# The first stage of a decoder block: eight token blocks side by side in place of five, with the modulation summed on VectorE

## The chip, the cores and the metric

The kernel runs on one core of a Trainium2 chip. A core has TensorE (PE, matrix products into PSUM), VectorE (DVE), ScalarE (ACT), GpSimd (POOL) and SyncE (SP), which here issues the DMAs. The metric is the device time of one execution in microseconds (us). Beside the runs that give the median, one execution was profiled; its trace gives all rows shown here.

## The reference

One decoder block for 1024 tokens with 1024 features, all in float32. This is the part that matters here:

```python
cond = silu(c)
sh_a, sc_a, gt_a, sh_m, sc_m, gt_m = split(cond @ w_ada + b_ada, 6)
h = rms_norm(x, g_attn_pre) * (1 + sc_a) + sh_a
proj = h @ w_in        # 1024 x 2304: q, k, v of two attention mixers
# rotary, sliding-window attention, dilated attention, out projection, gate, residual, then an MLP
```

`cond` is one vector of 1024 numbers, so `cond @ w_ada` for the shift and the scale of the first half of the block is a sum over 1024 rows of 2 x 1024 weights (8 MB). Shift and scale are wanted with the feature index on the partitions, since h is used transposed.

## The kernel before, in words

**Layout.** The tokens are cut into eight blocks (tb) of 128, the features into eight chunks (k) of 128, the columns of `w_in` into six units (u) of 384. Products keep float32 accuracy by a split: each operand is a high part (fp32r) and a low part (the rest), and three products are added: hi·hi, hi·lo (`proj_mm`, `part` 0, L771 and L772) and lo·hi (`part` 1, L774). A block of a unit is thus 24 products of 384 columns into one bank of PSUM. The split of h is `hw`, that of the weights `w_hl`.

**The first stage.** Each block of x is loaded (L449), its sum of squares taken on ScalarE (L553), the root by a pow on GpSimd (L412), x scaled (L558), transposed by eight TensorE products (L568), and copied to `xnT` (L573), features on partitions. `mod_chunk(k)` gets shift and scale of one chunk: the rows of `w_ada` lie eight to a partition, and the eight slices, each times its number of `cond`, are added over j and then over the partitions. For chunk 0 TensorE does all eight slices, for the others two (table `ADA_PE`, narrow products of one column, L615); VectorE adds the other six (`acc_a`, 128x256, L626 and L628), and two narrow products with ones add over the partitions (`pm`, L635). Then `g_a` and `s_a` (L640, L641), the modulation on ScalarE (L645), its high part on ScalarE (L651) and its low part on GpSimd (L654), for the first five blocks (`FIRST`) at once, 128x640. The weights of unit 0 are split on ScalarE (L473) and GpSimd (L478). The last three blocks go another way: their x is loaded when the last condition tiles have been issued, and modulation is done on the transposes (L583).

**Unit 0.** `first_unit` runs chunk by chunk over five blocks in five banks of PSUM, so that a chunk can be used as soon as it is modulated. Blocks 5 to 7 of unit 0 and the other units go block by block (`proj_tile`). Behind each block `evac` empties its bank: v to `v_hl` (L684, L689), rotary (L700 to L704), the split q and k (`sp`, `sk`, L716 and L717), transposed back by products with an identity.

**Behind it.** Attention of the heads already projected is woven into units 1 to 5; then come the out projection (461 to 565 us) and an MLP with seven products of half-size matrices (565 to 1186 us).

**The order.** All instructions come out of a list planner (`Sched`) that runs before the launch: steps with an estimated duration, dependencies, and rings of slots (`Res`) that they take and give. For each engine it picks the step that can start first, so a step's place on its engine follows from these estimates; on TensorE `prefer` ranks the streams. On the chip each engine runs its list in that order.

Of the kernel before, what the change touches and what calls it, by code (L numbers as in the profile page):

```python
# [19 lines left out]
P = 128  # L20
# [114 lines left out]
class Sched:  # L135


    def __init__(self):
        self.clk = dict(PE=0.0, ACT=0.0, DVE=0.0, POOL=0.0, SP=0.0)
        self.queue = {e: [] for e in ("ACT", "DVE", "POOL", "SP")}  # L140
        self.pe = {}
        self.launch = []
        self.seq = 0
        self.dma = 0.0

# [84 lines left out]
    def run(self, prefer):  # L230
        while True:
# [29 lines left out]
            if e == "PE":  # L261
                self.pe[name].pop(0)
# [41 lines left out]
def hybrid_block(ctx: ExitStack, tc: tile.TileContext, x, positions, w_ada, b_ada, g_attn_post, w_in, w_out,  # L304
# [110 lines left out]
    FIRST = 5  # L415
# [4 lines left out]
    xnT = p0.tile([P, KC, FIRST * P], F32, name="xnT")  # L420
    r_wa, r_xs, r_acc = Res(4), Res(2), Res(3)
# [6 lines left out]
    e_c = load(lambda: nc.sync.dma_start(head[:], consts[:, 0:HEAD]), 106496, prio=pri())  # L428
    wa_t, wa_e, sent = {}, {}, {}

    def load_ada(k):
        def emit():
            wa_t[k] = p0.tile([P, KC, 2, P], F32, name="wa", tag="wa", bufs=4)
            for i in range(2):
                nc.sync.dma_start(wa_t[k][:, :, i], ada_view[:, :, i * D + k * P:i * D + (k + 1) * P])

        def issued():
            sent[k].t = 0.0
        sent[k] = Ev()
        wa_e[k] = load(emit, 1048576, takes=[(r_wa, 1)], prio=pri(), after=issued)  # L440
# [3 lines left out]
    def load_x(tb, deps=()):  # L444
        r = r_stg if tb % 2 == 0 else r_xs

        def emit():
            x_t[tb] = stage("x_sb") if tb % 2 == 0 else p0.tile([P, D], F32, name="x_sb", tag="x_sb", bufs=2)
            nc.sync.dma_start(x_t[tb][:], x[tb * P:(tb + 1) * P])  # L449
        x_e[tb] = load(emit, 524288, deps, takes=[(r, 1)], prio=pri())  # L450
# [3 lines left out]
    def load_w(u, k, prio=None, deps=()):  # L454
# [13 lines left out]
        w_rawe[u, k] = load(emit, 196608, deps, takes=[(r_wst, 1)], prio=pri() if prio is None else prio)  # L468

    def split_w(u, k):  # L470
# [10 lines left out]
        if u == 0:  # L481
            w_e[u, k] = op("POOL", t_ptt(UW), lo(G), [e], gives=[(r_wst, 1)], prio=3)
# [3 lines left out]
    for tb in range(2):  # L486
        load_x(tb)
    e_posi = load(lambda: nc.sync.dma_start(posi[:], positions), 4096, prio=pri())
    load_ada(0)
    for tb in range(2, FIRST):  # L490
        load_x(tb)
    load_w(0, 0)
    for k in range(1, KC):
        load_ada(k)
        load_w(0, k)
    for tb in range(FIRST, TB):
        load_x(tb, [sent[KC - 2 if tb == FIRST else KC - 1]])

    e_init = op("DVE", 0.3, lambda: (V.memset(ones[:], 1.0), V.memset(nhalf[:], -0.5)), prio=0)
# [33 lines left out]
    def f_ang():  # L533
        V.tensor_scalar(ang[:], ang[:], 3.1415925, -3.1415925, ALU.min, ALU.max)
        V.tensor_scalar(kq[:], ang[:], -1.0, None, ALU.mult)
        V.tensor_tensor(kq[:], kq[:], ang[:], ALU.max)
        V.tensor_scalar(kq[:], kq[:], -1.0, float(np.pi / 2), ALU.mult, ALU.add)
    e = op("DVE", 0.8, f_ang, [e], prio=8)

    def f_sin():  # L540
# [3 lines left out]
    e = op("ACT", 3.0, f_sin, [e], prio=8)  # L544
    e_rope = op("DVE", 0.15, lambda: V.tensor_scalar(sinw[:, :, 0], sinw[:, :, 1], -1.0, None, ALU.mult), [e],
                prio=8)

    e_xn = []

    def x_block(tb):  # L550
# [8 lines left out]
        box, eh, d_all, evs_ = {}, [], [], []  # L559

        def hv():
            return x_t[tb][:].rearrange("p (k t) -> p k t", k=KC)
        r_x_ = r_stg if tb % 2 == 0 else r_xs
        for g in range(2):
# [4 lines left out]
            d = pe_op("xt", 0.7, tr, [e], takes=[(r_t, 1)], gives=[(r_x_, 1)] if g and tb < FIRST else [])  # L569
            d_all.append(d)  # L570
            if tb < FIRST:
                def ev(fn, g=g):
                    return lambda: fn(xnT[:, 4 * g:4 * g + 4, tb * P:(tb + 1) * P], box[g][:])  # L573
                e_xn.append(op("ACT", t_ps(512), ev(A.copy), [d], gives=[(r_t, 1)], prio=2))
            else:
                def ev(eng, g=g):
                    def f():
                        for k in range(4 * g, 4 * g + 4):
                            if eng is A:
                                A.activation(hv()[:, k], box[g][:, k - 4 * g], AF.Identity,  # L580
                                             bias=s_a[:, k:k + 1], scale=g_a[:, k:k + 1])
                            else:
                                V.tensor_scalar(hv()[:, k], box[g][:, k - 4 * g], g_a[:, k:k + 1],  # L583
                                                s_a[:, k:k + 1], ALU.mult, ALU.add)
                    return f
                evs_.append((d, ev))
        for d, ev in evs_:

            eh.append(op(("ACT", "DVE"), (1.4, 1.3), (ev(A), ev(V)), d_all + [e_gs[k] for k in range(KC)],
                         gives=[(r_t, 1)], prio=1))  # L590
        if tb >= FIRST:
            def hi(fn):
# [1357 lines left out]
```

## Time and profile before

| | |
|---|---|
| median of 3 runs | 1200.22 us (1197.69 to 1201.38) |
| profiled execution | 1197.14 us, span of the trace 1195.4 us |
| TensorE busy in the span | 96% |
| first product of block 5 of unit 0 | 77.18 us |
| first product of unit 2 | 174.97 us |

In the rows, L771 is line 771 of the kernel before; the fields are engine, operation, output<-inputs, shape. PE is TensorE's products, PEld its weight loads, which overlap. Rows of a timeline begin with the start in us and the busy time. Groups end with their count, the busy time and the mean of one in ns, then the idle time ahead of them with what ended it. A product's busy time spans its pipeline; the distance from start to start is its price in a row of products.

### The profile page before, as it was taken

The page shows a single profiled execution, that of the slowest core. Times are in us where ns is not written, and L with a number is a line of the kernel's source. Part 1 is how long each engine was busy: PE and PEld are TensorE (multiplying, and loading weights), DVE is VectorE, ACT ScalarE, POOL GpSimd, SP SyncE. Part 2 cuts the span into 40 slices and gives each one's busy share as a digit, 9 for nine tenths or more (in the row PEclk, how much of TensorE's full clock was granted, in tenths as well). Part 3 has the DMA queues.
Part 4 walks back from the last instruction along what each step waited for, and adds up shares of the span by engine and source line. Part 5 has one row for each costly group of instructions (what it writes and reads, how often), then busy time and mean ns, then how long its engine had stood idle before and what let it go on. Part 6 is the DMA issues. An engine that isn't in the chain of part 4 may idle for free.

```text
span 1195.4 us, 17424 instructions
## 1 busy us (share of the span) xinstructions
PE 1143.5 (96%) x6064; PEld 998.0 (83%) x6064; DVE 881.3 (74%) x1794; ACT 666.6 (56%) x1411; POOL 264.6 (22%) x325
## 2 busy tenths in 40 slices
PE   7879999999998998999899999999999999999996
PEld 6869999989998896888688888888888888888885
DVE  4977667666789897667888955479763797646998
ACT  6457666556666787667657533473325643246542
POOL 6534655465655333111100000000000000000002
PEclk9889999999999999999999999999999999999999
DMA  9621333213231422555296126952268511586103
GB/s 290 189 60 60 89 98 97 77 52 102 76 87 54 125 53 77 179 201 204 113 381 246 36 73 238 340 168 62 81 218 284 191 36 53 179 287 220 36 19 141
DMA packets 104423, 166.53 MB, mean 139 GB/s; under 512 B 11152, under 2 KB 56336, under 8 KB 104336
## 3 DMA queue, kind: packets, MB, share of 16 engines
q1 hardware_dynamic: 104336, 165.42, 41.8%
q8 instruction: 48, 0.79, 0.3%
q14 instruction: 39, 0.32, 0.1%
HBM read 137.08 MB, written 28.31 MB: 138 GB/s over the span
## 4 chain that ended last, share of the span: by engine, by line
PE 76%; DVE 13%; issue 4%; ACT 3%; POOL 3%; DMA 1%; SPq 0%; DVEq 0%; POOLq 0%; ACTq 0%
PE mlp_ps L1773 16%; PE mlp_ps L1774 16%; PE mlp_ps L1772 16%; PE pj L771 4%; PE pj L774 3%; PE pj L772 3%; PE s_ps L997 3%; PE o_ps L1131 1%; PE pt_ps L1100 1%; DVE acc_a L628 1%; PE y_ps L1348 1%; PE y_ps L1350 1%; PE pm L615 1%; PE y_ps L1349 1%; PE pt_ps L1103 1%
## 5 line engine op out<-in xcount | busy, mean ns | idle before, releaser
L1772 PE MATMUL mlp_ps<-hw 128*128 128x512 f32 x896 | 350.4, 391 | 0.4 <-ACT hw L1534 0.4
L1773 PE MATMUL mlp_ps<-hw 128*128 128x512 f32 x896 | 349.2, 390 | 1.1 <-DVE hw L1540 1.1
L1774 PE MATMUL mlp_ps<-hw 128*128 128x512 f32 x896 | 349.1, 390 | 0.0
L1773 PEld LDWEIGHTS mlp_ps<-hw 128*128 128x128 f32 x896 | 168.6, 188 | 36.9 <-DVE hw L1540 1.4
L1772 PEld LDWEIGHTS mlp_ps<-hw 128*128 128x128 f32 x896 | 168.6, 188 | 36.1 <-ACT hw L1534 0.8
L1774 PEld LDWEIGHTS mlp_ps<-hw 128*128 128x128 f32 x896 | 168.5, 188 | 35.1
L1543 DVE TENSOR_TENSOR hw<-w,hw 128x1024 fp32r<-128x1024 f32 x96 | 114.6, 1219 | 93.5 <-ACT hw L1536 93.3
L1536 ACT CAST hw<-w 128x1024 fp32r<-128x1024 f32 x96 | 97.4, 1046 | 129.9 <-PE mlp_ps L1774 93.2
L1872 POOL TENSOR_TENSOR st<-st,nhalf 128x1 f32<-128x1 f32 x8 | 7.8, 978 | 602.8 <-DVE st L1870 602.8
L771 PE MATMUL pj<-w_hl,hw 128*128 128x384 f32 x344 | 128.2, 373 | 10.0 <-DVE sk L717 10.0
L774 PE MATMUL pj<-w_hl,hw 128*128 128x384 f32 x344 | 117.4, 341 | 0.0
L772 PE MATMUL pj<-w_hl,hw 128*128 128x384 f32 x344 | 117.1, 341 | 0.0
L1536 ACT CAST hw<-u 128x1024 fp32r<-128x1024 f32 x48 | 48.6, 1051 | 64.6 <-PE mlp_ps L1774 64.6
L1118 DVE TENSOR_TENSOR ph<-pt_ps,ph 128x512 fp32r<-128x512 f32 (+1 forms) x110 | 68.8, 643 | 18.5 <-ACT ph L1114 17.6
L771 PEld LDWEIGHTS pj<-w_hl,hw 128*128 128x128 f32 x344 | 65.8, 191 | 11.8 <-issue 8.7
L1543 DVE TENSOR_TENSOR hw<-u,hw 128x1024 fp32r<-128x1024 f32 x48 | 57.0, 1217 | 18.2 <-ACT hw L1536 18.2
L1114 ACT CAST ph<-pt_ps 128x512 fp32r<-128x512 f32 (+1 forms) x110 | 59.2, 560 | 13.8 <-PE pt_ps L1103 9.8
L772 PEld LDWEIGHTS pj<-w_hl,hw 128*128 128x128 f32 x344 | 66.2, 192 | 0.8 <-issue 0.2
L774 PEld LDWEIGHTS pj<-w_hl,hw 128*128 128x128 f32 x344 | 65.7, 191 | 0.0
L1027 POOL TENSOR_SCALAR p_sb<-p_sb,den 128x128 f32<-128x128 f32 (+3 forms) x64 | 50.1, 786 | 70.2 <-DVE den L1025 46.8
L1830 DVE TENSOR_TENSOR yacc<-yacc,mlp_ps 128x512 f32<-128x512 f32 x96 | 62.1, 680 | 3.3 <-PE mlp_ps L1774 3.3
L1022 ACT ACTIVATE p_sb<-p_sb,mn 128x128 f32<-128x128 f32 (+3 forms) x64 | 49.9, 780 | 20.4 <-DVE mn L1015 16.6
(209 smaller groups left out, 2202.6 us busy)
## 6 DMA issues: line engine op xcount, KB each, us to landing
hw<-s_dram SPq DMA_DIRECT2D x84, 512.0 KB, 4.5
wa_st<-in_w_ada SPq DMA_DIRECT2D x32, 512.0 KB, 4.0
w<-in_w_up SPq DMA_DIRECT2D x32, 512.0 KB, 5.4
w<-in_w_down SPq DMA_DIRECT2D x32, 512.0 KB, 8.0
s_dram<-hw SPq DMA_DIRECT2D x28, 512.0 KB, 4.3
x_sb<-in_x SPq DMA_DIRECT2D x16, 512.0 KB, 6.2
wa<-in_w_ada SPq DMA_DIRECT2D x16, 512.0 KB, 7.0
w_st<-in_w_in SPq DMA_DIRECT2D x32, 192.0 KB, 4.7
```

The lines of the kernel that those rows point to most:

```text
L771: T.matmul(ps, hw[:, tb, 0, t], w[:, 0], start=(k == 0), stop=False)
L772: T.matmul(ps, hw[:, tb, 0, t], w[:, 1], start=False, stop=False)
L774: T.matmul(ps, hw[:, tb, 1, t], w[:, 0], start=False, stop=(k == KC - 1))
L1027: lambda b=b, qi=qi: G.tensor_scalar(rec.p[qi], rec.p[qi], b["den"][:], 1.0, ALU.mult, ALU.mult), [e], prio=1))
L1114: A.copy(b["ph"][:, 0, :w], b["pt"][:, :w])
L1118: V.tensor_tensor(b["ph"][:, 1, :w], b["pt"][:, :w], b["ph"][:, 0, :w].bitcast(F32), ALU.subtract)
L1536: A.copy(out[j][0], flat(src[j]))
L1543: V.tensor_tensor(out[j][1], flat(src[j]), out[j][0].bitcast(F32), ALU.subtract)
L1772: T.matmul(ps[m][:], sh, mh, start=starts and k == 0, stop=False, **kw)
L1773: T.matmul(ps[m][:], sh, ml_, start=False, stop=False, **kw)
L1774: T.matmul(ps[m][:], sl, mh, start=False, stop=k == 3, **kw)
L1830: e = op("DVE", t_dv(512), lambda: V.tensor_tensor(y(), y(), ps[m][:], ALU.add), [e, ml.e_y[tb, n]], gives=gives, prio=1)
```

## The change

Only the first stage and unit 0 are written anew.

- `FIRST` is 8: all eight blocks of x are loaded early, turned to `xnT`, and accumulate unit 0 side by side in all eight banks of PSUM. The list `order0` sets the order of the loads, and `in_turn` issues each behind the one before.
- The modulation goes by four groups of two chunks. A group has four tiles of 0.5 MB, two j and 2 x 256 columns each; every third of the tiles and x blocks uses the staging ring, the others a ring of six.
- The sums over j are on VectorE alone, 128x512 (L611, L613 of the changed kernel), eight instructions for a group; four narrow products add over partitions (L621). `ADA_PE` and its products are gone.
- ScalarE writes the high part straight from the modulation (L649); VectorE does the modulation again in full (L647) and subtracts (L652). The first group is done in two halves of four blocks, the others over all eight, 128x1024.
- The weights of unit 0 are split on VectorE in place of GpSimd. GpSimd keeps the steps of the rotary angle, the pow, and six low parts of unit 1's weights. The rest of the angle follows behind the x blocks.
- `filler` puts products of 128x512 ones into TensorE's list where the planner sees it idle, until block 4 (`FILL`), whose bank they write, begins; its first product starts the sum anew.
- Unit 0 runs over seven blocks for chunks 0 to 5 (`AHEAD` is 6), then block 7 for these, then each block's chunks 6 and 7. The weights of unit 1 are loaded as soon as the first stage's loads are out.

```diff
-    FIRST = 5
+    FIRST = 8
+    AHEAD = 6
+    order0 = [("x", 0), ("x", 1)] + [(0, j) for j in range(4)] + [("x", t) for t in range(2, 4)] + [("w", 0), ("w", 1)] + [("x", t) for t in range(4, TB)] + [a for g in range(1, 4) for a in [(g, j) for j in range(4)] + [("w", 2 * g), ("w", 2 * g + 1)]]
...
         if u == 0:
-            w_e[u, k] = op("POOL", t_ptt(UW), lo(G), [e], gives=[(r_wst, 1)], prio=3)
+            w_e[u, k] = op("DVE", t_dv(UW), lo(V), [e], gives=[(r_wst, 1)], prio=3)
...
+    def mod_group(g):
+        b = {}
+        e = e_cond
+        c = slice(2 * g, 2 * g + 2)
+        for j in range(4):
             def f(j=j):
...
+                for n in range(2):
+                    w, cj = wa_t[g, j][:, 512 * n:512 * n + 512], cond[:, 2 * j + n:2 * j + n + 1]
+                    if j == n == 0:
+                        b["acc"] = p0.tile([P, 512], F32, name="acc_a", tag="acc_a", bufs=2)
+                        V.tensor_scalar(b["acc"][:], w, cj, None, ALU.mult)
+                    else:
+                        V.scalar_tensor_tensor(b["acc"][:], w, cj, b["acc"][:], ALU.mult, ALU.add)
...
+        for half in ((0, 1) if g == 0 else (None,)):
+            for k in range(2 * g, 2 * g + 2):
+                mod_chunk(k, eg, half)
+        for k in range(2 * g, 2 * g + 2):
+            split_w(0, k)
...
+        eh = op("ACT", t_sb(n) + 2 * AP_COST, lambda: A.activation(hh, h, AF.Identity, bias=s_a[:, k:k + 1],
+                                                                  scale=g_a[:, k:k + 1]), deps, prio=0)
+        e = op(("DVE", "ACT"), (t_d2(n) + 2 * AP_DV, t_sb(n) + 2 * AP_COST), (full(V), full(A)), [eh], prio=0)
+        e = op("DVE", t_dv(n), lambda: V.tensor_tensor(hw[:, t0:t1, 1, ks], h, hh.bitcast(F32), ALU.subtract), [e],
+               prio=0)
...
-    acc_at = [(pj, "pj", r_pj)] * 2 + [(po, "o", r_o)] + [(psp, "s", r_s)] * 2
+    acc_at = [(pj, "pj", r_pj)] * 2 + [(po, "o", r_o)] + [(psp, "s", r_s)] * 2 + [(pt, "t", r_t)] * 2 + [(px, "x", r_x)]
...
+    def filler(start, o):
+        if fill.open or e_init.t is None:
+            return
+        idle = start - max(sc.clk["PE"], e_init.t + 0.2)
+        n = int(max(0.75 * idle, 0.5 * min(o.dur, 2.0)) / 0.22)
+        for _ in range(n):
+            T.matmul(accs[FILL][:], ones_r[:, :P], ones_r[:], start=True, stop=True)
+        sc.clk["PE"] += max(0.0, 0.22 * n - max(0.0, idle))
...
     def first_unit():
+        order = [(k, part, tb) for x in (0, 1) for k in range(2) for part in range(2)
+                 for tb in (range(4) if x == 0 else range(4, 7))]
+        order += [(k, part, tb) for k in range(2, AHEAD) for part in range(2) for tb in range(7)]
+        order += [(k, part, 7) for k in range(AHEAD) for part in range(2)]
+        order += [(k, part, tb) for tb in (7, 0, 1, 2, 3, 4, 5, 6) for k in range(AHEAD, KC) for part in range(2)]
```

The order of VectorE's instructions in the sums, before, about two chunks (`acc_a` the sums, `pm` the totals, `bb` the bias):

```order
L626 TENSOR_SCALAR acc_a<-wa,cond 128x256
L640 TENSOR_SCALAR g_a<-pm,bb,head 128x1
L641 TENSOR_SCALAR s_a<-pm,bb 128x1
L628 SCALAR_TENSOR_TENSOR acc_a<-wa,cond,acc_a 128x256 x3
L620 TENSOR_TENSOR bb<-bb,pm 128x2
L628 SCALAR_TENSOR_TENSOR acc_a<-wa,cond,acc_a 128x256 x2
```

And VectorE at the end of the changed first stage, from the middle of the last group's sums (`w_hl` the weight splits, `xnT` the modulation, `hw` the low parts, chunk 4's first):

```order
L613 SCALAR_TENSOR_TENSOR acc_a<-wa,cond,acc_a 128x512 x2
L509 TENSOR_TENSOR w_hl<-w_st,w_hl 128x384
L647 TENSOR_SCALAR xnT<-xnT,g_a,s_a 128x1024
L613 SCALAR_TENSOR_TENSOR acc_a<-wa,cond,acc_a 128x512 x2
L652 TENSOR_TENSOR hw<-xnT,hw 128x8x128 x2
L627 TENSOR_TENSOR g_a<-pm,bb 128x2
L628 TENSOR_TENSOR g_a<-g_a,head 128x2
L629 TENSOR_TENSOR s_a<-pm,bb 128x2
L509 TENSOR_TENSOR w_hl<-w_st,w_hl 128x384 x2
...
L647 TENSOR_SCALAR xnT<-xnT,g_a,s_a 128x1024 x2
L652 TENSOR_TENSOR hw<-xnT,hw 128x8x128 x2
```

The sums, the splits of weights and the low parts, three engines' work before, now stand in one list.

GpSimd's list in the same stage, before:

```order
L478 TENSOR_TENSOR w_hl<-w_st,w_hl 128x384
L654 TENSOR_TENSOR hw<-xnT,hw 128x5x128 x2
L478 TENSOR_TENSOR w_hl<-w_st,w_hl 128x384
L654 TENSOR_TENSOR hw<-xnT,hw 128x5x128
L478 TENSOR_TENSOR w_hl<-w_st,w_hl 128x384
L654 TENSOR_TENSOR hw<-xnT,hw 128x5x128
```

And of the changed kernel, from the last steps of the angle to unit 1's weights:

```order
L565 TENSOR_TENSOR ang<-ang,km 128x64
L564 TENSOR_SCALAR km<-kq 128x64
L416 TENSOR_TENSOR rstd<-rs_t,nhalf 128x1
L565 TENSOR_TENSOR ang<-ang,km 128x64
L416 TENSOR_TENSOR rstd<-rs_t,nhalf 128x1 x4
L509 TENSOR_TENSOR w_hl<-w_st,w_hl 128x384 x6
```

All low parts of h and of unit 0's weights have left GpSimd.

TensorE where the two lists become the same, before (the pv products L1131 and L1136, probabilities turned L1100 and L1103, unit 2 or 3's products between):

```order
L1131 MATMUL o_ps<-ph,v_hl 128x256 x2
L1136 MATMUL o_ps<-ph,v_hl 128x256 x2
L1100 MATMUL pt_ps<-head,p_sb 128x128 x2
L1103 MATMUL pt_ps<-head,p_sb 128x128
L771 MATMUL pj<-w_hl,hw 128x384
L772 MATMUL pj<-w_hl,hw 128x384
L774 MATMUL pj<-w_hl,hw 128x384
L997 MATMUL s_ps<-kt,qt 128x128 x2
```

And in the changed kernel, the lines shifted by 34 or 4:

```order
L1165 MATMUL o_ps<-ph,v_hl 128x256 x2
L1170 MATMUL o_ps<-ph,v_hl 128x256 x2
L1134 MATMUL pt_ps<-head,p_sb 128x128 x2
L1137 MATMUL pt_ps<-head,p_sb 128x128
L775 MATMUL pj<-w_hl,hw 128x384
L776 MATMUL pj<-w_hl,hw 128x384
L778 MATMUL pj<-w_hl,hw 128x384
L1031 MATMUL s_ps<-kt,qt 128x128 x2
```

From the first of these rows, at 275.50 us before, nothing moves on TensorE to the end.

More of the change, by code (lines that the diff above doesn't have):

```diff
@@ L660, in hybrid_block, with ev @@
[L660 to L665 removed]
+            d = pe_op("xt", 0.43, tr, [e], takes=[(r_t, 1)], gives=[(r_x_, 1)] if g else [])
+            def ev(fn, g=g):
+                return lambda: fn(xnT[:, 4 * g:4 * g + 4, tb * P:(tb + 1) * P], box[g][:])
+            e_xn[tb // 4].append(op(("ACT", "DVE"), (t_ps(512), t_dv(512)), (ev(A.copy), ev(V.tensor_copy)), [d],
+                                    gives=[(r_t, 1)], prio=2))
@@ new lines, in hybrid_block, with f_ang @@
+    for tb in range(TB):
+        x_block(tb)
+    for g in range(4):
+        mod_group(g)
+    def f_ang():
+        V.tensor_scalar(ang[:], ang[:], 3.1415925, -3.1415925, ALU.min, ALU.max)
+        V.tensor_scalar(kq[:], ang[:], -1.0, None, ALU.mult)
+        V.tensor_tensor(kq[:], kq[:], ang[:], ALU.max)
+        V.tensor_scalar(kq[:], kq[:], -1.0, float(np.pi / 2), ALU.mult, ALU.add)
+    e = op("DVE", 0.8, f_ang, [e_ang] + e_xn[0] + e_xn[1], prio=8)
+    e = op("ACT", 3.0, f_sin, [e], prio=8)
@@ L777, in tick @@
         st.d += 1 / (TB * KC)
[L779 to L794 removed]
+    FILL, accs = 4, {}
```

258 lines of the change are left out of this document (114 added, 144 removed).

## The prediction

> **What bounds the kernel now.** I read the busy shares and the chain of waits first, then the stages' windows: each engine's busy time, TensorE's granted clock (PEclk), the DMA engines' share, GB/s.
>
> ```profile
> PE 1143.5 (96%) x6064; PEld 998.0 (83%) x6064; DVE 881.3 (74%) x1794; ACT 666.6 (56%) x1411; POOL 264.6 (22%) x325
> PE 76%; DVE 13%; issue 4%; ACT 3%; POOL 3%; DMA 1%; SPq 0%; DVEq 0%; POOLq 0%; ACTq 0%
> ...
> core 0: us, PE busy (x) PEld busy (x) DVE busy (x) ACT busy (x) POOL busy (x), PEclk, DMA share, GB/s
> 0.00:30.00 30.00, 21.39 (x96) 20.12 (x97) 13.88 (x37) 18.07 (x30) 18.12 (x42) 1.00 1.04 290
> 30.00:60.00 30.00, 26.72 (x149) 25.44 (x147) 27.03 (x54) 14.74 (x24) 16.21 (x12) 0.89 0.66 187
> 60.00:80.00 20.00, 12.12 (x67) 11.18 (x68) 17.53 (x58) 9.22 (x32) 7.50 (x6) 0.84 0.29 82
> 80.00:112.00 32.00, 30.37 (x210) 29.08 (x209) 21.62 (x81) 22.96 (x77) 13.94 (x19) 0.94 0.20 61
> 112.00:280.00 168.00, 164.07 (x1174) 158.54 (x1173) 118.55 (x408) 105.59 (x314) 91.61 (x99) 0.99 0.29 83
> 565.00:1186.00 621.00, 615.75 (x2709) 507.74 (x2708) 455.47 (x508) 297.71 (x408) 12.45 (x9) 1.00 0.46 163
> ```
>
> From 80 us on TensorE is 95% busy or more: nothing there can be won by moving work between the other engines. Before that it isn't the bound. It did 149 instructions in 30 to 60 us and 67 in 60 to 80, against 210 in the 32 us behind, while VectorE was 90% and 88% busy. So the first 80 us are a VectorE stage. The timeline of TensorE (start, busy time, then the wait ahead of it in brackets) and SyncE's waits say how:
>
> ```profile
> 29.49 0.52 PE L771 MATMUL acc<-w_hl,hw 128*128 128x384 f32 x1
> 29.81 0.52 PE L772 MATMUL acc<-w_hl,hw 128*128 128x384 f32 x1
> ...
> 63.16 0.33 PE L771 MATMUL acc<-w_hl,hw 128*128 128x384 f32 x1
> 63.33 0.33 PE L772 MATMUL acc<-w_hl,hw 128*128 128x384 f32 x1
> ...
> 77.18 0.66 PE L771 MATMUL pj<-w_hl,hw 128*128 128x384 f32 x1 [5.56 <-DVE sk L717]
> 79.58 0.52 PE L771 MATMUL pj<-w_hl,hw 128*128 128x384 f32 x1
> 79.90 0.52 PE L772 MATMUL pj<-w_hl,hw 128*128 128x384 f32 x1
> ...
> 275.50 0.40 PE L1131 MATMUL o_ps<-ph,v_hl 128*128 128x256 f32 x2
> ...
> SPq L848 <- DVE acc_a L628: 17.5, 1, 17.5
> ```
>
> A product of 384 columns starts 0.32 us behind its neighbour at 29.5 and at 79.6, and 0.17 at 63.2: at the start, and again behind the pause of 5.56 us, TensorE runs at half its rate. SyncE stood 17.5 us on one sum before it could send for the last x blocks. At 77.18 unit 0 has five of its eight blocks done.
>
> **The change, and what it costs.** By the order of instructions TensorE's list from the pv product at 275.50 us to its end is the same before and after. So I need only one number: how much earlier that product comes. I work out when unit 1 begins (T1), and from there to the marker.
>
> *The marker.* Before, 77.18 to 275.50 is 198.3 us. It holds three blocks of unit 0 that the change has done before T1: 3 x 24 products by 0.172 = 12.4. It also holds the half rate at 77 to 80.4, about 1.6. So T1 + 184.3 is the new marker, and the gain is 275.5 - 184.3 - T1 = 91.2 - T1.
>
> *The first group.* The first four x blocks, the first four condition tiles and VectorE's reductions:
>
> ```profile
> 4.70 1.06 ACT L553 ACTIVATE junk<-x_sb 128x1024 bf16<-128x1024 f32 x1 [1.69 <-DMA x_sb<-in_x]
> ...
> 9.53 0.59 ACT L573 COPY xnT<-pxt 128x512 f32<-128x512 f32 x1 [0.27 <-PE pxt L568]
> ...
> 10.00:15.00 5.00, 5.00 (x26) 5.00 (x25) 0.95 (x2) 3.77 (x7) 3.78 (x12) 1.00 1.06 377
> 25.00:30.00 5.00, 4.01 (x16) 3.95 (x17) 4.08 (x8) 4.74 (x7) 3.78 (x6) 1.00 1.17 290
> ```
>
> x0 is there at 4.70. Behind it come seven transfers of 0.524 MB until the fourth x block: 3.67 MB at 290 to 377 GB/s take 9.7 to 12.7, so it lands at 14.4 to 17.4. From landing to the copied transposes took 10.12 - 4.70 = 5.4 before. With 0.7 for ScalarE's half modulation and 1 for the angle steps on GpSimd ahead of the block's pow, VectorE begins to split the first half group at 21.5 to 24.8; I take 23, at some 330 GB/s.
>
> *VectorE from there.* The rows nearest to each operation (shortest, median and longest in ns, or busy time and mean):
>
> ```profile
> L884 DVE SCALAR_TENSOR_TENSOR ada_acc<-wa_st,cond,ada_acc x14: 742/751/753, 662.9 to 816.5; 128x512 f32<-128x512 f32 x14
> L882 DVE TENSOR_SCALAR ada_acc<-wa_st,cond x2: 480/483/486, 662.4 to 752.2; 128x512 f32<-128x512 f32 x2
> L1118 DVE TENSOR_TENSOR ph<-pt_ps,ph 128x512 fp32r<-128x512 f32 x78 | 52.2, 682 | 14.0 <-ACT ph L1114 13.2
> L558 DVE TENSOR_SCALAR x_sb<-x_sb,rstd x8: 745/764/2043, 6.7 to 64.0; 128x1024 f32<-128x1024 f32 x8
> L1543 DVE TENSOR_TENSOR hw<-w,hw 128x1024 fp32r<-128x1024 f32 x96 | 114.6, 1219 | 93.5 <-ACT hw L1536 93.3
> L478 DVE TENSOR_TENSOR w_hl<-w_st,w_hl x16: 539/596/1482, 107.5 to 388.9; 128x384 fp32r<-128x384 f32 x16
> 71.68 0.22 DVE L700 TENSOR_TENSOR ra<-acc,cosw 128x64 f32<-128x64 f32 x1
> ```
>
> Three groups of sums, each one multiply (0.48) and seven multiply-adds (0.75): 17.2. The first pair's halves: four modulations at 0.48 and four subtractions at 0.68, 4.6. Five modulations of 1024 at 0.76, 3.8, and six subtractions at 1.22, 7.3. Six weight splits at 0.60, 3.6; three groups of small operations and the angle steps at about 0.2 each, 2.6; one x block scaled, 0.8. Together 39.9. Behind chunk 4's subtraction stand 7.7 of it (three subtractions 3.7, two modulations 1.5, two weight splits 1.2, small ones 1.4), so that subtraction is out at 23 + 32.2 = 55.2 and VectorE is through at 62.9.
>
> *TensorE from there.* Behind chunk 4's subtraction stand 7 lo·hi products of chunk 4, 21 of chunk 5, block 7's 18 for chunks 0 to 5, then 48 for chunks 6 and 7: 94 by 0.172 = 16.2, to 71.4. It needs VectorE's last piece at about 64, so that lies hidden by a microsecond; if this cover goes, each microsecond costs one. The products of ones end when block 4 begins; the pauses on group 3's sums behind it are open, and I add one stretch at half rate, 1.7, bounds 0 to 4. **T1 = 73.1, gain 18.1 us.**
>
> *What I cost at nothing, and why.* The narrow products of before:
>
> ```profile
> L615 PE MATMUL pm<-cond,wa 128*128 128x1 f32 x88 | 15.7, 305 | 1.1 <-DVE s_a L641 1.1
> L635 PE MATMUL pm<-ones,acc_a 128*128 128x1 f32 x28 | 4.2, 255 | 4.4 <-DVE acc_a L628 3.1 <-DVE rs_t L409 1.2
> L478 POOL TENSOR_TENSOR w_hl<-w_st,w_hl 128x384 fp32r<-128x384 f32 x32 | 33.4, 1056 | 33.0 <-ACT w_hl L473 32.8
> ```
>
> TensorE loses 88 products of the first kind, 15.7 us of busy time, but stood idle for VectorE in 30 to 80 anyway; I count nothing for them. The products of ones stand in TensorE's queue ahead of transposes and products that wait for VectorE or x anyway; without that cover the 20 at the start would cost 20 x 0.43 = 8.6 at half rate. That 0.43 is an estimate, 512/384 of 0.32. Six of unit 1's weight splits go to GpSimd, 6 x 1.06 = 6.3, and are wanted only from T1 on; if they came late, unit 1 would wait for up to that. The loads now go out strictly in turn, so a tile that waits for a free slot holds all behind it on SyncE's queue, unit 1's weights last; a slot comes free with a tile's sums, in VectorE's own order, so this adds nothing while VectorE sets the pace. Unit 0's eight banks of PSUM must be emptied in a row as unit 1 starts; that lies beside unit 1's products (rival below).
>
> *DMA.* 14.3 MB are loaded by unit 0. At 290 GB/s the second group's first tile comes at 27.8, when VectorE is done with its first half group at 26.8: with the later start, T1 is about 4 later, gain 14; at 377 T1 is 1.5 earlier. The pieces have rows of 1 KB, whose rate no row shows; below about 275 GB/s the last tile decides.
>
> *GpSimd off.* The same sum at half the width, and GpSimd's two operations beside it:
>
> ```profile
> L628 DVE SCALAR_TENSOR_TENSOR acc_a<-wa,cond,acc_a x35: 467/485/1785, 21.1 to 60.4; 128x256 f32<-128x256 f32 x35
> L628 DVE SCALAR_TENSOR_TENSOR acc_a<-wa,cond,acc_a 128x256 f32<-128x256 f32 x35 | 26.6, 759 | 0.8
> L654 POOL TENSOR_TENSOR hw<-xnT,hw 128x640 fp32r<-128x640 f32 x8 | 13.4, 1677 | 13.3 <-ACT hw L651 13.3
> ```
>
> The sum takes 485 ns in the median and 759 in the mean, up to 1785, where GpSimd works beside it. At the median 35 would take 17.0, so 9.6 of VectorE's time was loss. Between the ends 0.75 and 0.75 x 759/485 = 1.17 for the new wide sums I take 0.75, since nothing but the angle steps and pow is left on GpSimd until unit 1's weights.
>
> [...]
>
> **Rivals.**
> *Larger gain.* Transfers at 377 GB/s and no half rate: T1 69.9, gain 21.3. Behind T1 the windows hold more that could go: in 80 to 112 us 1.6 idle and 32 x 0.06 = 1.9 at the lower clock, in 112 to 280 3.9 idle, 7.4 in all; gain up to 28: 1172. Against it: the later waits belong to attention, which the change doesn't touch, and the clock was lowered in every window of 30 to 112.
> *Contention stays* (angle steps, unit 1's weights): 24 sums by 1.17 in place of 0.75, +10: T1 83, gain 8, 1192. For it: the mean; against it: L654 is gone.
> *The clock isn't held.* If the open pauses leave the whole tail at half rate, 94 by 0.32 = 30.1, T1 = 85.3: gain 6, 1194. For it: half rate behind the 5.56 us pause; against: the tail has no pause once it runs.
>
> [...]
>
> *Given back behind T1.* Emptying a block is six small VectorE operations, an estimated 1.9 us by the 0.22 row: 8 x 1.9 = 15 us; if TensorE's unit 1 waits for all of it, gain 3: 1197, no change. Against it: unit 1's first block needs one free bank, and block 0, whose bank it takes, is done six blocks of 6 products (6.2 us) before T1.
> *Slower.* VectorE's sums are the place: at the worst row's surcharge, 1.785 - 0.485 = 1.3 each, 24 cost 31, T1 104, 13 us slower: 1213. It decides from 18.1/24 = 0.75 us extra for each. For it: alone on VectorE, all sums lie on the path; against it: one in 35 only was that long.
>
> **How the numbers follow.** The profiled execution took 1197.14 us with a span of 1195.4; the median of the runs is 1200.22, 3.1 above it. 1197.1 - 18.1 = 1179.0 beside the profile, 1182 beside the median. Chances: forecast (gain 12 to 25) 0.66, larger 0.08, contention 0.10, clock 0.05, given back 0.05, slower 0.06. Faster is the forecast, larger, contention and clock: 0.89; same 0.05; slower 0.06. A change under 0.3% (3.6 us) can't be told from none here. The range 1168 to 1196 holds all but given back and slower, with 4 us beside larger and 2 beside the clock for the bounds left over; the forecast alone is 1175 to 1188.
>
> **What would show it.** Right: the first product of unit 1 at 70 to 77 us; wide sums near 0.75 us; the pv product of 275.5 at 257; 0.17 us between products in 56 to 71. Wrong: sums above 1 us (contention); VectorE idle on condition tiles at 27 to 50 (DMA); 0.32 between products behind 60 (clock); waits of the pj products on sk or v_hl behind T1 (given back).

## The result and the profile after

The changed kernel takes 1186.65 us in the median of four runs (1184.34 to 1188.11), the one before 1198.95 beside it: ratio 0.9894, 95% interval 0.9866 to 0.9921, 12.3 us less. A second comparison on another chip (below) gave 0.9870 (0.9853 to 0.9887), 15.5 us. Forecast were 18.1.

The page's busy shares and the shares of the chain of waits, then the windows of the stages, of the changed kernel:

```profile
PE 1144.4 (96%) x6043; PEld 993.0 (84%) x6043; DVE 883.2 (74%) x1791; ACT 662.8 (56%) x1394; POOL 240.0 (20%) x307
PE 73%; DVE 14%; issue 4%; ACT 4%; POOL 3%; DMA 1%; SPq 0%; DVEq 0%; POOLq 0%; ACTq 0%
...
0.00:30.00 30.00, 24.67 (x111) 19.48 (x112) 16.90 (x43) 16.82 (x29) 15.62 (x39) 0.89 0.97 325
30.00:60.00 30.00, 26.68 (x152) 24.18 (x151) 29.50 (x48) 16.31 (x25) 4.42 (x4) 0.94 0.61 185
60.00:80.00 20.00, 18.69 (x111) 17.73 (x110) 17.38 (x68) 13.73 (x43) 8.17 (x9) 1.00 0.38 116
80.00:112.00 32.00, 30.06 (x233) 29.12 (x232) 24.61 (x97) 22.60 (x75) 13.90 (x18) 1.00 0.20 57
```

VectorE is busy 29.50 of 30 us in 30 to 60; GpSimd 4.42 in place of 16.21. In 60 to 80 TensorE does 111 instructions in place of 67.

The marks of the forecast, on TensorE's timeline (start, busy time, wait ahead): the first product of unit 0, a pause, chunk 4's low part, the first product of unit 1, and the pv product from which the lists are the same:

```profile
27.15 0.42 PE L775 MATMUL acc<-w_hl,hw 128*128 128x384 f32 x1
...
54.49 0.69 PE L775 MATMUL acc<-w_hl,hw 128*128 128x384 f32 x1 [1.21 <-ACT hw L649]
54.97 0.52 PE L776 MATMUL acc<-w_hl,hw 128*128 128x384 f32 x1
55.29 0.52 PE L775 MATMUL acc<-w_hl,hw 128*128 128x384 f32 x1
...
59.25 0.95 PE L778 MATMUL acc<-w_hl,hw 128*128 128x384 f32 x4
...
78.86 0.33 PE L775 MATMUL pj<-w_hl,hw 128*128 128x384 f32 x1
...
260.98 0.40 PE L1165 MATMUL o_ps<-ph,v_hl 128*128 128x256 f32 x2
```

Unit 1 begins at 78.86 (forecast 73.1), the marker comes at 260.98 in place of 275.50: 14.5 us won there. Of these the profiled execution has 9.2 at its end (span 1186.2 in place of 1195.4). By the same products of TensorE's list, the lead over the kernel before is 14.1 at 365 us, 12.4 at 376, 10.9 at 412 and 9.2 at 500. The clock column has a stretch at a lower clock at each of these steps; the windows before, and below them after:

```profile
370.00:380.00 10.00, 8.41 (x56) 7.81 (x55) 8.97 (x28) 6.28 (x22) 4.48 (x6) 1.00 0.25 68
400.00:410.00 10.00, 10.00 (x70) 9.65 (x69) 8.55 (x32) 9.32 (x31) 4.92 (x10) 1.00 0.37 106
440.00:450.00 10.00, 9.60 (x65) 8.56 (x63) 9.31 (x31) 8.45 (x31) 1.86 (x4) 1.00 0.12 28
```

```profile
370.00:380.00 10.00, 10.00 (x63) 9.73 (x62) 8.89 (x34) 6.85 (x27) 3.43 (x5) 0.83 0.17 41
400.00:410.00 10.00, 8.24 (x44) 7.48 (x44) 8.02 (x31) 7.12 (x23) 3.01 (x8) 0.83 0.22 67
440.00:450.00 10.00, 6.56 (x29) 4.97 (x28) 7.93 (x22) 7.41 (x23) 6.74 (x10) 0.66 0.46 133
```

TensorE was granted 0.83, 0.83 and 0.66 of its clock there, before 1.00 each time. The second profile of the changed kernel has such windows at the same places (0.89, 0.83 and 0.52). In the first profile products of 384 columns stood 0.32 us apart in 371.6 to 374.6 and in 405.9 to 408.7, and 0.17 between. The windows lie where TensorE's list is the same; what sets them off is open. That the clock takes the last step, too, isn't shown: the run below with the angle steps behind all eight blocks was granted 1.00 from 370 to 460 us and still lost 2.9 of its lead behind 440 us, where TensorE waited for ScalarE (1.85 at 444.70, for `oh`).

VectorE and GpSimd about the start of the first split, of the changed kernel:

```profile
15.75 0.15 DVE L413 TENSOR_SCALAR rs_t<-ssq 128x1 f32<-128x1 f32 x1 [0.57 <-ACT junk L579]
...
19.80 0.75 DVE L584 TENSOR_SCALAR x_sb<-x_sb,rstd 128x1024 f32<-128x1024 f32 x1 [2.98 <-POOL rstd L416]
...
27.60 0.99 DVE L647 TENSOR_SCALAR xnT<-xnT,g_a,s_a 128x512 f32<-128x512 f32 x2
...
57.74 2.35 DVE L652 TENSOR_TENSOR hw<-xnT,hw 128x1024 fp32r<-128x1024 f32 x2
```

```profile
13.79 0.78 POOL L565 TENSOR_TENSOR ang<-ang,km 128x64 f32<-128x64 f32 x1
14.65 0.63 POOL L564 TENSOR_SCALAR km<-kq 128x64 f32<-128x64 f32 x1
15.36 0.32 POOL L565 TENSOR_TENSOR ang<-ang,km 128x64 f32<-128x64 f32 x1
15.77 0.24 POOL L564 TENSOR_SCALAR km<-kq 128x64 f32<-128x64 f32 x1
...
18.95 0.32 POOL L565 TENSOR_TENSOR ang<-ang,km 128x64 f32<-128x64 f32 x1
19.22 0.55 POOL L416 TENSOR_TENSOR rstd<-rs_t,nhalf 128x1 f32<-128x1 f32 x1
```

The third x block's pow is wanted at 15.9 and done at 19.77: nineteen angle steps stand between the second block's pow and this one in GpSimd's list, the last eleven from 15.4 to 19.3. They are late themselves. While VectorE adds the first group (until 15.2) a step takes 0.56 to 0.78 us, behind it, until 19.2, 0.24 to 0.32. The six sums from 10.51 on took 4.67 us, 0.78 each, against a median of 0.752: in this stretch it is GpSimd that was slowed. So VectorE begins its first split at 27.60. From there to the end of its last low part, at 65.95, it has no wait.

### The profile page after: what moved, and what is told of

The parts are those of the page before. It is cut to its first block, busy times and chain, and to the rows that moved or that the text cites. A ratio compares the mean times of both kernels' runs of the same rounds, so it can differ in the third digit from the quotient of the medians.

```text
span 1186.2 us, 17403 instructions
## 1 busy us (share of the span) xinstructions
PE 1144.4 (96%) x6043; PEld 993.0 (84%) x6043; DVE 883.2 (74%) x1791; ACT 662.8 (56%) x1394; POOL 240.0 (20%) x307
## 4 chain that ended last, share of the span: by engine, by line
PE 73%; DVE 14%; issue 4%; ACT 4%; POOL 3%; DMA 1%; SPq 0%; DVEq 0%; POOLq 0%; ACTq 0%
PE mlp_ps L1807 16%; PE mlp_ps L1806 16%; PE mlp_ps L1808 16%; PE pj L775 4%; PE pj L778 3%; PE pj L776 3%; PE s_ps L1031 2%; PE o_ps L1165 1%; DVE ph L1152 1%; PE pt_ps L1134 1%; PE y_ps L1382 1%; PE y_ps L1384 1%; PE y_ps L1383 1%; DVE hw L1577 1%; PE pt_ps L1137 1%
## 5 line engine op out<-in xcount | busy, mean ns | idle before, releaser
L775 PE MATMUL pj<-w_hl,hw 128*128 128x384 f32 x320 | 118.8, 371 | 1.9 <-DVE sk L721 1.8
L778 PE MATMUL pj<-w_hl,hw 128*128 128x384 f32 x320 | 109.4, 342 | 0.0
L776 PE MATMUL pj<-w_hl,hw 128*128 128x384 f32 x320 | 109.0, 341 | 0.0
L1148 ACT CAST ph<-pt_ps 128x512 fp32r<-128x512 f32 (+1 forms) x110 | 58.9, 558 | 21.0 <-PE pt_ps L1137 15.8
L775 PEld LDWEIGHTS pj<-w_hl,hw 128*128 128x128 f32 x320 | 61.1, 191 | 3.0 <-DVE sk L721 2.3
L776 PEld LDWEIGHTS pj<-w_hl,hw 128*128 128x128 f32 x320 | 61.4, 192 | 0.7 <-POOL w_hl L509 0.2
L778 PEld LDWEIGHTS pj<-w_hl,hw 128*128 128x128 f32 x320 | 61.0, 191 | 0.0
L1056 ACT ACTIVATE p_sb<-p_sb,mn 128x128 f32<-128x128 f32 (+3 forms) x64 | 49.8, 778 | 13.9 <-DVE mn L1049 12.3
```

The source lines that it names most:

```text
L775: T.matmul(ps, hw[:, tb, 0, t], w[:, 0], start=(k == 0), stop=False)
L776: T.matmul(ps, hw[:, tb, 0, t], w[:, 1], start=False, stop=False)
L778: T.matmul(ps, hw[:, tb, 1, t], w[:, 0], start=False, stop=(k == KC - 1))
L1056: A.activation(rec.p[qi], rec.p[qi], AF.Exp, bias=b["mn"][:, m:m + 1], scale=-1.0, accum_out=b["den"][:])
L1148: A.copy(b["ph"][:, 0, :w], b["pt"][:, :w])
```

## The experiments

The last three kernels start from the one before, the others from the changed one. Where they share TensorE's list from the pv product on, that product ("the marker") and the first product of unit 1 are read beside the time, since the clock windows behind the marker differ between executions (0.66 and 0.52 at 440 to 450 us in the two profiles of the changed kernel). The kernel before took 1199.76, 1198.92, 1200.57 and 1200.29 us beside the four sets of runs, so times of different sets compare to 1 or 2 us.

**The angle steps behind the first four x blocks.**

```diff
-    e = e_pos
-    for f in steps:
-        e = op("POOL", 0.34, f, [e, e_c], prio=8)
...
     for tb in range(TB):
         x_block(tb)
+    e = e_pos
+    for f in steps:
+        e = op("POOL", 0.34, f, [e, e_c] + e_xn[0], prio=8)
```

> The changed kernel with GpSimd's 36 angle steps made to wait for the copies of the first four x blocks, so that the pow of these blocks stands ahead of them. My theory: VectorE began its first split at 27.60 and not at 23 because the pow of the third x block, wanted at 15.8, stood behind angle steps on GpSimd until 19.2. Then the first split comes at 23 to 24, unit 1 begins at 74.5 to 75.5 in place of 78.86, and the time falls by 3 to 5 us. Rival: the x blocks or the next condition tiles land too late in any case; then the first split stays above 26.5, or VectorE waits on tiles behind it, and the time moves by less than 1.5 us.

1187.68 us: nothing won. The first split came at 24.45, 3.15 earlier and close to the 23 to 24 expected, yet unit 1 began at 80.02. VectorE's timeline and GpSimd's show where it went:

```profile
33.57 0.69 DVE L591 COPY xnT<-pxt 128x512 f32<-128x512 f32 x1 [2.34 <-PE pxt L587]
34.18 1.59 DVE L609 SCALAR_TENSOR_TENSOR acc_a<-wa,cond,acc_a 128x512 f32<-128x512 f32 x2
36.88 0.69 DVE L591 COPY xnT<-pxt 128x512 f32<-128x512 f32 x1 [1.11 <-PE pxt L587]
```

```profile
29.92 0.63 POOL L564 TENSOR_SCALAR km<-kq 128x64 f32<-128x64 f32 x1
30.62 1.02 POOL L416 TENSOR_TENSOR rstd<-rs_t,nhalf 128x1 f32<-128x1 f32 x1
```

The pow of the seventh block stood behind the moved steps, and VectorE waited 2.34 + 1.11 = 3.45 for the transposes of the last two blocks.

**The angle steps behind all eight.** Against the run above:

```diff
-        e = op("POOL", 0.34, f, [e, e_c] + e_xn[0], prio=8)
+        e = op("POOL", 0.34, f, [e, e_c] + e_xn[0] + e_xn[1], prio=8)
```

> As the run with the angle steps behind the first four blocks, but behind the copies of all eight. There the first split came 3.1 us earlier, and was given back when VectorE waited 3.45 us for the transposes of x6 and x7, whose pow stood behind the angle steps. My theory: with all eight pow ahead, VectorE has no such wait, its last low part ends at 63 to 64, unit 1 begins at 75.5 to 77, and the time is 2 to 4 us below that of the changed kernel. Rival: the angle steps, now beside the sums, end too late, and VectorE waits for them at its angle operations near 58 us, 2 us or more: nothing won.

The first split came at 23.26, VectorE had no wait above 0.5 us from there to the end of its last low part at 62.84, and unit 1 began at 75.80, the marker at 256.2. The split is 4.3 earlier, nearly the 4.6 that my forecast missed, and 3.1 of it reached unit 1. The time is 1184.88 us (six runs), 1.8 below the changed kernel's first median and 0.2 below its second: its trace is earlier, but a gain in the time is not shown. I had expected 2 to 4 us.

**VectorE's second modulation on ScalarE, too.** Against the run above:

```diff
-        e = op(("DVE", "ACT"), (t_d2(n) + 2 * AP_DV, t_sb(n) + 2 * AP_COST), (full(V), full(A)), [eh], prio=0)
+        e = op("ACT", t_sb(n) + 2 * AP_COST, full(A), [eh], prio=0)
```

> As the run with the angle steps behind all eight blocks, and the second modulation in full on ScalarE, too: VectorE's list is 4 x 0.48 + 5 x 0.76 = 5.7 us shorter. If VectorE's list is the path, unit 1 begins at 73 to 75.5, TensorE being the bound from there as with half of the sums, and the time falls by another 1 to 3 us. Rival: on ScalarE the two modulations of a pair take 4.8 us behind the sums in place of 3.2, so the last low part comes no earlier: unit 1 at 76 to 79, nothing won.

1183.86 us, unit 1 at 74.46. VectorE's last low part ended at 63.45, no earlier than without the edit (62.84): the rival's mechanism, VectorE waiting 4.9 us for ScalarE at its last pair. Unit 1 came 1.3 earlier nevertheless, which neither theory has; the time moved by 1.0, within the spread.

**Half of the sums of groups 1 to 3.** On the changed kernel; it leaves out one of the two slices of each tile:

```diff
-                for n in range(2):
+                for n in range(2 if g == 0 else 1):
```

> The changed kernel with half of the sums of groups 1 to 3 left out: of each tile's two slices only the first is added (12 multiply-adds of 0.75 us fewer on VectorE, all tiles still loaded). My theory: VectorE's list is the path until unit 0's last chunks, so the last low part ends 9 us earlier than 65.95, at 57 to 58; TensorE then has no more pauses to give (some 6 us of waits and half rate between 34 and 78 us) and becomes the bound: unit 1 at 72 to 75 in place of 78.86, the time 4 to 7 us shorter. Rival, the tiles' landing sets the pace: VectorE waits on tiles for most of the 9 us, last low part behind 62, unit 1 within 2 us of 78.86.

VectorE's last low part ended at 57.25 (8.7 earlier than 65.95), unit 1 began at 74.35, 4.5 earlier, and the time was 1184.10: 2.5 below the changed kernel's first median and 1.0 below its second, where 4 to 7 were expected. VectorE's list is the path; about half of what is taken from it comes out at unit 1, then TensorE is the bound, its waits from 40 us on being 0.3 and one of 1.8 for the emptying of unit 0, beside products at half rate in 67.5 to 70.6.

**The low parts on GpSimd again.**

```diff
-            w_e[u, k] = op("DVE", t_dv(UW), lo(V), [e], gives=[(r_wst, 1)], prio=3)
+            w_e[u, k] = op("POOL", t_ptt(UW), lo(G), [e], gives=[(r_wst, 1)], prio=3)
...
-        e = op("DVE", t_dv(n), lambda: V.tensor_tensor(hw[:, t0:t1, 1, ks], h, hh.bitcast(F32), ALU.subtract), [e],
+        e = op("POOL", t_ptt(n), lambda: G.tensor_tensor(hw[:, t0:t1, 1, ks], h, hh.bitcast(F32), ALU.subtract), [e],
```

> The changed kernel with the low parts of h and of unit 0's weights on GpSimd again. VectorE is relieved of 4 x 0.64 + 6 x 1.18 + 8 x 0.52 = 13.8 us of subtractions, GpSimd gets about 4 x 1.4 + 6 x 2.7 + 8 x 1.06 = 30 us. Theory of contention: VectorE's sums beside them rise from 0.75 to 1.0 us or more in the mean, and GpSimd's last low parts end behind 66 us: unit 1 is 2 to 8 us later than 78.86. Rival, VectorE's list is all that counts: sums stay near 0.75, unit 1 up to 8 us earlier.

1198.07 us: the whole gain is gone. Beside the kernel before the ratio is 0.9985 (0.9968 to 1.0002), so without this part the rest of the change is worth nothing that these runs can tell. Unit 1 began at 88.33, the marker came at 270.7. The sums and the subtractions by form, of this run, and below them the sums of the changed kernel by their source line (shortest, median, longest):

```profile
L613 DVE SCALAR_TENSOR_TENSOR acc_a<-wa,cond,acc_a 128x512 f32<-128x512 f32 x28 | 29.7, 1060 | 0.7
L652 POOL TENSOR_TENSOR hw<-xnT,hw 128x1024 fp32r<-128x1024 f32 x6 | 16.1, 2690 | 11.0 <-DVE xnT L647 11.0
...
L613 DVE SCALAR_TENSOR_TENSOR acc_a<-wa,cond,acc_a x28: 737/752/2775, 8.6 to 62.4; 128x512 f32<-128x512 f32 x28
```

```profile
L613 DVE SCALAR_TENSOR_TENSOR acc_a<-wa,cond,acc_a x28: 737/752/1379, 9.1 to 56.4; 128x512 f32<-128x512 f32 x28
```

A sum takes 752 ns in the median in both, but up to 2775 here, where GpSimd's subtractions take 2.69 us. The mean goes from 0.77 to 1.06, 28 x 0.29 = 8.1 us on VectorE, against which 13.8 us of subtractions left it. So the slower sums alone don't explain the delay. Other steps of VectorE slowed as well (a modulation of 0.81 took 2.71), and the planner gave it three copies to `xnT` more, 2.1 us. The subtractions stand on the path too: the last two take 2.4 us each on GpSimd, 1.2 on VectorE, and the last ended at 76.14, in place of 65.95. What each of these costs isn't separated.

The traces show slower steps on both sides: up to 2.78 us for a sum of 0.75 in this run, and up to 0.78 for an angle step of 0.32 in the changed kernel.

**Five blocks ahead, two whole at the end.**

```diff
-        order += [(k, part, tb) for k in range(2, AHEAD) for part in range(2) for tb in range(7)]
+        order += [(k, part, tb) for k in range(2, AHEAD) for part in range(2) for tb in range(5)]
...
+        order += [(k, part, tb) for tb in (5, 6) for k in range(KC) for part in range(2)]
```

> The changed kernel with five blocks in place of seven ahead of block 7, and blocks 5 and 6 of unit 0 whole at the end. Work is the same; 28 more of the products stand behind chunk 4's low part (122 in place of 94). My theory: those of before had room beside VectorE's list, so unit 1 begins 28 x 0.172 = 4.8 us later, 83 to 84, and the time rises by 4 to 5.5 us, less what the earlier blocks' emptying gives back. Rival: eight side by side has no worth of its own, since TensorE is behind in any case; unit 1 within 1.5 us of 78.86.

1193.87 us, 7.2 above the changed kernel; unit 1 at 88.09, 9.2 later, the marker at 268.6, 7.6 later. That is more than the 4.8 of the products, which I had expected: TensorE's granted clock was 0.75 in 39 to 60 us, in place of 0.92, and its products ran at half rate from 54.8 to 62.9 (0.32 us apart). So seven blocks side by side put work beside VectorE's sums. That they also keep TensorE's rate up through them rests on this one profile.

**Without the products of ones.**

```diff
-    sc.filler = filler
+    sc.filler = None
```

> The changed kernel without the products of ones; nothing else moves on any engine. My theory: VectorE's list sets the end of the first stage, TensorE's early products lie beside it at either rate, and unit 1 begins within 0.7 us of 78.86. Rival: without them TensorE is at half rate in 27 to 45 us, the products of chunks 2 and 3 are late by 0.15 us each, and TensorE is still behind when chunk 4's low part is there: unit 1 2 to 4 us later.

1186.47 us, the same. Unit 1 began at 80.25, 1.4 later, half of it a later first split (28.38): more than the 0.7 of my theory, less than the 2 of the rival. The marker came at 260.1, 0.9 earlier. In this order of work the ones are worth nothing that can be measured.

**GpSimd off alone, on the kernel before.** Run twice.

```diff
-            w_e[u, k] = op("POOL", t_ptt(UW), lo(G), [e], gives=[(r_wst, 1)], prio=3)
+            w_e[u, k] = op("DVE", t_dv(UW), lo(V), [e], gives=[(r_wst, 1)], prio=3)
...
-        e_hl[k] = op("POOL", t_ptt(NF0), lo(G), [e_hh[k]], prio=0)
+        e_hl[k] = op("DVE", t_dv(NF0), lo(V), [e_hh[k]], prio=0)
```

> The kernel before with one part of the change: the low parts of h and of unit 0's weights on VectorE in place of GpSimd. VectorE gets about 8 x 0.75 + 8 x 0.52 = 10 us more and loses the excess of its sums, 35 x (0.759 - 0.485) = 9.6 us. My theory: the two cancel, unit 0's sixth block begins within 3 us of 77.2 and the time is the same within 0.3%. Rival: GpSimd was what was waited for (its low parts ended the chunks), and taking it off brings most of the gain by itself: 6 us or more.

1188.60 us, ratio 0.9907 (0.9873 to 0.9941): 10.3 won, where I had expected nothing. The sums fell from 759 ns to 483 in the mean, and block 5 of unit 0 began at 64.17 in place of 77.18. VectorE's 16 subtractions took 11.0 us and its sums 35 x 0.276 = 9.7 less. So by these two its list isn't shorter, as I had counted. But a subtraction of a low part of h takes 0.82 us in the mean there, in place of 1.68 on GpSimd, and the last ended at 58.5 in place of 67.3. How much the quicker subtractions bring and how much the freed sums isn't separated. And the five runs spread from 1182.78 to 1193.12, so it was run again beside the changed kernel.

> The changed kernel once more, on one chip with the two runs below, since the medians of separate calls differ by about 1 us. Both theories: 1185 to 1188 us.

> The kernel before with only its low parts of h and of unit 0's weights moved to VectorE, again, beside the changed kernel on the same chip. New theory: taking GpSimd off the subtractions carries the change, and eight blocks, pairs and products of ones add nothing to it: 1183 to 1189 us, within 3 us of the changed kernel, pv product of 275.5 at 255 to 259. Rival: the rest of the change is worth several us by itself, and the first run of this kernel was lucky in its profile: 4 us or more slower than the changed kernel.

On one chip: changed 1185.07 (1184.23 to 1185.83), GpSimd off alone 1192.84 (1188.21 to 1195.81), before 1200.57. So GpSimd off alone is worth 7.7 us there, and the rest of the change 7.8 on top. My new theory, that the rest adds nothing, fell too. The two profiles of the same kernel differ by 6.7 us at block 5 (64.17 and 70.89), and TensorE's timelines tell why, first execution and second:

```profile
10.46 4.02 PE L615 MATMUL pm<-cond,wa 128*128 128x1 f32 x32
...
37.41 0.33 PE L771 MATMUL acc<-w_hl,hw 128*128 128x384 f32 x1
37.59 0.33 PE L772 MATMUL acc<-w_hl,hw 128*128 128x384 f32 x1
...
64.17 0.41 PE L771 MATMUL pj<-w_hl,hw 128*128 128x384 f32 x1 [2.68 <-DVE sk L717]
```

```profile
10.63 6.83 PE L615 MATMUL pm<-cond,wa 128*128 128x1 f32 x32
...
37.35 0.52 PE L771 MATMUL acc<-w_hl,hw 128*128 128x384 f32 x1
37.67 0.52 PE L772 MATMUL acc<-w_hl,hw 128*128 128x384 f32 x1
...
70.89 0.66 PE L771 MATMUL pj<-w_hl,hw 128*128 128x384 f32 x1 [2.69 <-DVE sk L717]
```

The same 32 narrow products took 4.02 us and 6.83, and products of 384 columns stood 0.18 and 0.32 us apart at 37 us. Unit 0's products stood 0.32 apart until 31 us in the one execution (0.17 from 32.40 on), until 43 in the other. VectorE's waits for the narrow products (`pm`) show how this reaches block 5, first execution and second:

```profile
32.32 0.16 DVE L620 TENSOR_TENSOR bb<-bb,pm 128x2 f32<-128x2 f32 x1 [1.06 <-PE pm L615]
34.78 0.16 DVE L620 TENSOR_TENSOR bb<-bb,pm 128x2 f32<-128x2 f32 x1 [0.31 <-PE pm L615]
```

```profile
35.14 0.16 DVE L620 TENSOR_TENSOR bb<-bb,pm 128x2 f32<-128x2 f32 x1 [1.75 <-PE pm L615]
39.73 0.16 DVE L620 TENSOR_TENSOR bb<-bb,pm 128x2 f32<-128x2 f32 x1 [2.43 <-PE pm L615]
42.51 0.28 DVE L640 TENSOR_SCALAR g_a<-pm,bb,head 128x1 f32<-128x1 f32 x1 [1.10 <-PE pm L635]
```

The first low part came at 28.53 and at 30.66, 2.1 later. From there to 48 us VectorE waited 1.6 us for `pm` in the first execution and 6.1 in the second: with the 2.1 that makes 6.6 of the 6.7. In these two executions, then, block 5 follows the rate at which TensorE ran.

**GpSimd off alone, with the products of ones.** On that kernel, with the `filler` called for each step of TensorE:

```diff
+        idle = start - max(sc.clk["PE"], e_init.t + 0.2)
+        n = int((0.75 if start < 9 else 1.3) * max(0.0, idle) / 0.22)
+        for _ in range(n):
+            T.matmul(accs[FILL][:], ones_r[:, :P], ones_r[:], start=True, stop=True)
```

> The kernel before with its low parts on VectorE, run twice until now, and only products of 128x512 ones added in TensorE's early pauses (47, none behind the first product of block 4; no other instruction moves). The two profiles of that kernel differ by 6.7 us at block 5 of unit 0 (64.17 and 70.89): the products of unit 0 were at half rate until 31 us in one and until 43 in the other. My theory: the granted rate, which differs from execution to execution, decides there, and the ones make it certain: full rate by 31 us at the latest, block 5 at 63 to 66, the time 1183 to 1188 us and its spread below 6 us. Rival: the rate is only a trace of something else that was late, or the ones only add to the queue: block 5 at 68 or later, 1190 us or more.

TensorE was at full rate from 20.7 us to 45 (eight narrow products in 0.95 us, in place of 1.71; products of 384 columns 0.17 apart at 28.8 and at 44.3), and block 5 came at 65.63, as expected. The time is 1188.72 us, 4.1 below the second measurement without them, on another chip, and 0.1 above the first; the runs still spread over 8.6 us (1185.36 to 1193.93), which I had not expected. Block 5 lies near the 64.17 of the first execution and far from the 70.89 of the second, as the theory of the rate has it. That the full rate came ten microseconds sooner than in the first brought nothing more. One profile doesn't show that the ones make the full rate certain, and the runs don't show a narrower spread.

**GpSimd off alone, angle steps behind the first five blocks.**

```diff
-    e = e_pos
-    for f in steps:
-        e = op("POOL", 0.34, f, [e, e_c], prio=8)
...
     for tb in range(FIRST):
         x_block(tb)
+    e = e_pos
+    for f in steps:
+        e = op("POOL", 0.34, f, [e, e_c] + e_xn, prio=8)
```

> The kernel before with its low parts on VectorE, and the angle steps behind the first five x blocks. If the third block's pow behind angle steps holds this order of work too, the first low part comes 2 to 3 us before 28.53, block 5 of unit 0 begins at 61 to 63 in place of 64.17, and the time falls by 1 to 3 us against the run without the second edit. Rival: here x5 to x7 and their modulation decide, which are loaded last; block 5 within 1 us of 64.17, no change.

1195.33 us: slower by 2.5 than without this edit on the same chip. The first low part came at 26.80, but block 5 only at 73.10: unit 0's products were at half rate until 38.5, and TensorE was at half rate again in 73.1 to 76.4 and 93.5 to 96.6. Neither theory has this: with such differences of rate between executions it can't be told from this run what the edit does.

## Why the prediction was right, and where it missed

The time lies in the range and in the forecast's own; the gain was two thirds to five sixths of the 18.1, and the smaller of its two measurements, 12.3, is just above 12, the forecast's lower end. Two of the signs that I had named were missed: unit 1 began at 78.86 and not at 70 to 77, and the pv product came at 260.98 and not at 257. The path, VectorE's list and TensorE behind it, was the right one; one term ahead of it was too small.

- **The first group: the step that failed.** I put the first split at 21.5 to 24.8 us (the terms shown add up to 24.5 at the late end), with 1 us for "the angle steps on GpSimd ahead of the block's pow"; it came at 27.60. The third block's pow was 3.3 us late (19.22 against 15.9), and behind it VectorE waited 0.5 to 1.2 four times more, for the next blocks' pow and transposes. That 1 us was a guess: I had counted neither the nineteen steps ahead of that pow, nor that beside the wide sums they take 0.56 to 0.78 us in place of 0.24 to 0.32. With the steps out of the way the split came at 23.26 (the run with all eight blocks ahead). The transfers came as taken: 325 GB/s in the first 30 us, between my bounds.
- **VectorE's list** was right: 32.2 us from the first split to chunk 4's low part, measured 58.9 - 27.6 = 31.3; to its end 39.9 against 38.35. The sums at 0.75 were 0.752 in the median, 0.772 in the mean: the surcharge by GpSimd, which I weighed as a mean up to 1.17, is 28 x 0.02 = 0.6 us.
- **TensorE behind it**: 17.9 us forecast, 78.86 - 59.25 = 19.6 measured. There was no half rate in it: the granted clock was 1.00 in 59 to 78.9. Half rate lay ahead, at 54.5 to 57.5 (clock 0.50, products 0.32 apart, behind the open pause on group 3's sums), where it cost nothing that VectorE's list did not cover. In its place stood 12 transposes of the blocks already emptied, and waits of 0.63 and 0.61 for them. That the two figures lie so near is luck: the 1.7 that I had added for half rate was an estimate that no run shows in this stretch. I had left the transposes in the stretch behind T1, which came out at 182.1 in place of 184.3: what T1 lost there the marker got back.
- **The sum at the marker**: 18.1 were forecast; 4.6 were lost at the start, 0.9 won in VectorE's list, 2.1 lost between chunk 4's low part and unit 1, and 2.2 got back behind it. That makes 14.5, as measured.
- **Behind the marker** I took the rest as unmoved. TensorE's list is, but its pace isn't: the first profile lost 4.9 of its lead between 365 and 500 us. Some 3.2 of it fell at two stretches at half rate; what took the rest, behind 440 us, is open. The 14.5 of the marker were 9.2 at that profile's end; over the runs 12.3 and 15.5 were left.
- **Contention**, a rival at 0.10, did not stay in the changed kernel: its wide sums took 0.772 us in the mean, not 1.17. The loss of 9.6 that I had read from the sums before is part of what the change removes. With the low parts put back on GpSimd the time is 11.4 us longer. I explained the gain by one list on VectorE; the runs show two things of like size, GpSimd off (7.7 to 10.3 alone, 11.4 taken back) and eight blocks side by side (7.2 taken back). They aren't parts of a sum: each is measured with the other's state given. With GpSimd off, the rest of the change was worth 7.8 on one chip; with the low parts on GpSimd, nothing that can be told from none.
- **The clock isn't held**, at 0.05, did not come to pass in the changed kernel, with or without ones: unit 1 began at 78.86 and 80.25, not at 85.3. In the kernel before with GpSimd off, 6.6 of the 6.7 us between two profiles at block 5 go with the rate.
- **Given back** and **slower** did not come to pass: unit 1's first product had no wait, and the stretch behind it was shorter than counted; the slowest sum was 1.38.
- **DMA**: VectorE had no wait on condition tiles behind 27.60, so the transfers did not hold its list.

## What to carry to other kernels

Before work is spread over a second engine, look at the mean beside the median of what the first one does meanwhile: 759 against 485 said that GpSimd's help cost VectorE's sums 9.6 us, about what the subtractions would cost there. When a step waits for a small operation on another engine, as VectorE did here for GpSimd's pow of 0.55 us, count what stands ahead of it in that engine's list, at the price it has beside the new neighbours, not the old: here nineteen angle steps, 0.56 to 0.78 us beside the wide sums and 0.24 to 0.32 without them. And a step moved out of one block's way must be moved out of the way of all: behind four blocks it won 3.15 us and gave back 3.45.

## What the runs showed of the hardware that I had not expected

- TensorE's rate in the first 45 us differed between two executions of one kernel: unit 0's products 0.32 us apart until 31 us in one, until 43 in the other, 6.7 us at block 5 of unit 0. The clock column shows 1.00 in 30 to 45 us of the second, while its products stand 0.32 us apart until 43: there the distance of products is the safer reading.
- VectorE and GpSimd were both slower side by side: a 128x64 step on GpSimd went from 0.24 to 0.32 us up to 0.56 to 0.78 beside wide sums, a sum of 0.75 us up to 2.78 where GpSimd's subtractions took 2.69.
- Windows at half rate came at 370 to 410 us in both profiles of the changed kernel (granted clock 0.83 at 370 to 380 and 0.83 at 400 to 410, 0.89 and 0.83 in the second), and not in the one before (1.00 from 360 to 450) nor in the run with the angle steps behind all eight, with the same list on TensorE. The two of them took 1.7 and 1.5 us of the lead in the first profile, 1.0 and 1.5 in the second.
